# SSM preparation moved between the tiles of a feed-forward block, and a weight request moved into the down projection before it

## The chip, the cores and the metric

The kernel runs on one core of a Trainium2 chip. TensorE (PE) multiplies matrices, and its weight loads are shown apart as PEld; VectorE (DVE), ScalarE (ACT) and GpSimd (POOL) work element by element, and SyncE (SP) issues most of the DMAs. Each engine takes its own queue in order, and semaphores tie the queues together. The metric is the device time of one execution in microseconds (us); lower is better.

## What is computed

One layer of a hybrid decoder: a SwiGLU block at half weight, then a mixer in which an SSM and an attention run side by side, then a second SwiGLU block, and a last norm. 512 tokens, 1024 channels, 2816 inner channels, all float32.

```python
def swiglu(h, w_gate, w_up, w_down):
    return (jax.nn.silu(h @ w_gate) * (h @ w_up)) @ w_down

h = rms_norm(x, ffn1_norm[l])
x = x + RES_HALF * swiglu(h, ffn1_w_gate[l], ffn1_w_up[l], ffn1_w_down[l])
h = rms_norm(x, mix_norm[l])
...
x = x + y @ w_out[l]
h = rms_norm(x, ffn2_norm[l])
x = x + RES_HALF * swiglu(h, ffn2_w_gate[l], ffn2_w_up[l], ffn2_w_down[l])
```

The SSM needs matrices that depend on its parameters alone: powers of a complex decay, an input matrix, an output matrix and a matrix for short distances. The kernel works these out on the chip, beside FFN 1.

## The kernel before

**Precision.** Each float32 operand is split into a high part (`hi`, `whi`: a cast on ScalarE) and the rest (`lo`, `wlo`: a subtraction on VectorE). `mm3` (L198) makes a product of three matmuls: high by high at L200, high weight by low input at L201, low weight by high input at L202. A weight so passes a DMA to `wraw`, a cast to `whi`, a subtraction to `wlo`. `wraw`, `whi` and `wlo` have three buffers each, so a cast can start when TensorE has finished with the weight three before it.

**Groups.** Each FFN takes its 22 inner tiles in four groups, of 6, 6, 6 and 4 tiles (counted here from 1). A group first multiplies by gate and up, then `down` (L446) multiplies by the down weights in eight steps m = 0 to 7, each one 128-channel tile of `x`. `down` asks for three weights ahead; the one for step m + 3 is asked for after the matmuls of step m. After each step VectorE adds to `x` (L458), and `after(m)` runs whatever else was planned there.

**Plain tiles and pairs.** Groups 1 and 2 of FFN 1, and group 1 of FFN 2, work tile by tile, gate and up in turn: twelve tiles (0 to 11) in a group, of 24 matmuls of 512 columns each. The other groups go by `pairs` (L589): a pair is two inner tiles worked together in a fast matrix scheme of seven products in place of eight. Seven steps (n = 0 to 6), for gate and up each, of 256 columns, take combined weights and combined inputs `xq` (named b11, b21, n2, t1, t3, b22, t4 in the order of the steps). `pair_weights` (L566) loads a pair's raw weights, for gate and up one `wraw` and two `wb` each, and adds four sums `s` on GpSimd (L575). `prepare(i)` (L599) asks for these at a pair's first step, and for each step casts `whi` (L609) and subtracts `wlo` (L610). It runs two steps ahead (`AHEAD`). Before the change the first two of a group were asked for when `pairs` began, so after the whole of the down before it. FFN 1 has three pairs in group 3 and two in group 4; FFN 2 has three, three and two in its groups 2 to 4.

**Planned beside it.** `SLOTS` lists, for every place in FFN 1 where `hidden` (L401) is called, which steps of three lists are taken: `e` and `l` are the early and late steps of the SSM preparation (`prep_steps`, L704), `p` is the preparation of the pairs' inputs (`quarters`, L461). Its third line holds the twelve tiles of group 2, its fourth the first seven steps of the down behind them. VectorE's part of a slot is ordered behind the last `wlo` (`self.low`) and the last activation (`self.acted`); GpSimd's part is not. The sixteen late steps are: one that starts the tables `ec` and `es` with three squarings on VectorE; six doublings (`double`, L1039), on GpSimd, each of which needs another squaring from VectorE (all but the last); one that loads `sC`; and eight `c_powers` (L1070), by turns on GpSimd and VectorE, three operations each (`tC`, `tC`, `mC`) and a store to `kC`. In `quarters`, the two `add` steps make the sums of inputs on GpSimd (`qe`, `qd`, `q2`, `q4`), and `combos` splits them into `xu`, `xm`/`xx`, `xq`. In FFN 2 the `after` of group 1's down (L697) takes the same kind of steps, the last of them `plain("b22")` at step 5, ordered behind `self.low`.

**Order.** The program's order is a priority. A planner with a simulated timeline lays out the queue of each engine from it: what is ready on the simulated engine goes first, and among these what stands first in the program. `issue_after` forces an order on one engine. `chained` (L582) keeps the casts, and the subtractions, of the pairs in the order of the steps.

Of the kernel before, what the change touches and what calls it, by code (L numbers as in the profile page):

```python
# [20 lines left out]
KT = D // P  # L21
# [11 lines left out]
FGROUPS = {1: ((0, 6), (6, 12), (12, 18), (18, 22)), 2: ((0, 6), (6, 12), (12, 18), (18, 22))}  # L33
# [4 lines left out]
NCL = {1: 12, 2: 6}  # L38
SLOTS = ("e|e|e|e||||e"
         "|p|p|p|p|p|p|e|e|e"  # L40
         "|el|eel|eel|eel|eel|eel|eel|eep|pl|ll|epl|l"
         "|pl|pl|l|l|||")
BY_TRANSFER = 99
RELOAD = (0, 1, 0, 1, 0, 1, 0, 1)
AHEAD = 2
# [96 lines left out]
class Body:  # L142
# [250 lines left out]
    def ffn1(self):  # L393
        wgu, wd = self.d["wgu1"], self.d["wd1"]
        early, late, reload = self.prep_steps()
        prep = self.quarters(1)
        names = {"e": early, "l": late, "p": prep}
        slots = [[names[q].pop(0) for q in step] for step in SLOTS.split("|")]
        assert not early and not late and not prep

        def hidden(_=None):  # L401
            if slots:
                with ExitStack() as late:
                    for i in (self.acted, self.low):
                        if i is not None:
                            late.enter_context(self.tc.issue_after(i.ins))
                    for f in slots.pop(0):
                        f()

        hooks = {(1, 1): self.first_norm, (2, 1): self.norm_bcast}  # L410
        for f0, f1 in FGROUPS[1]:
            last = f1 == NF
            if f0 >= NCL[1]:
                acts = self.pairs(1, range((f0 - NCL[1]) // 2, (f1 - NCL[1]) // 2))
            else:
                acts, pend = [], []
                for f in range(f0, f1):
                    if f == 0:
                        pend.append(self.first_pair(1, wgu, self.xg))
                        continue  # L420
                    pair = []
                    for gu in range(2):
                        wh, wl = self.weight(wgu[f, gu].rearrange("p k m -> p (k m)"), 1024, by_transfer=f >= BY_TRANSFER)
                        ps = self.ps("gu")
                        x = self.hn if f0 else self.xg
                        for k in range(KT):
                            self.mm3(ps, wh[:, k * P:(k + 1) * P], wl[:, k * P:(k + 1) * P], x[k][0], x[k][1],
                                     k == 0, k == KT - 1)
                        pair.append(ps)
                        hooks.get((f, gu), hidden)()  # L430
                    pend.append(pair)
                    while pend and f >= max(hooks)[0]:
                        acts.append(self.activate(*pend.pop(0), normed=f0 > 0))
                if f0 == 0:
                    hidden()
            if last:
                self.prenorm(self.g_mix)
                self.reload = reload

                def hidden(m):  # L440
                    self.prenorm_tile(m)
                    if RELOAD[m]:
                        reload.pop(0)()
            self.down(wd, f0, f1, acts, hidden)

    def down(self, wd, f0, f1, acts, after):  # L446
        nf = f1 - f0
        get = lambda m: self.weight(wd[m, :, f0:f1].rearrange("p k m -> p (k m)"), nf * P)
        ws = [get(m) for m in range(3)]
        for m in range(KT):  # L450
            wh, wl = ws[m]
            ps = self.ps("dn")
            for j in range(nf):
                self.mm3(ps, wh[:, j * P:(j + 1) * P], wl[:, j * P:(j + 1) * P], acts[j][0], acts[j][1],
                         j == 0, j == nf - 1)
            if m + 3 < KT:
                ws.append(get(m + 3))
            self.added = self.nc.vector.scalar_tensor_tensor(self.x[m], ps, 0.5, self.x[m], op0=ALU.mult, op1=ALU.add)  # L458
            after(m)

# [125 lines left out]
                st.enter_context(self.tc.issue_after(self.chain[key].ins))  # L586
            self.chain[key] = f()

    def pairs(self, layer, js):  # L589
        nc = self.nc  # L590
        V, A = nc.vector, nc.scalar
        xs = ("b11", "b21", "n2", "t1", "t3", "b22", "t4")
        bank = ("a", "b", "a", "c", "a", "c", "a")
        new = (1, 1, 0, 1, 0, 0, 0)
        steps = [(j, n) for j in js for n in range(7)]
        behind = lambda: ExitStack() if (layer, j) == (2, js[-1]) else self.tc.issue_after(self.chain["V"].ins)
        ws, parts, out = {}, {}, []

        def prepare(i):  # L599
            if i >= len(steps):  # L600
                return
            j, n = steps[i]
            if n == 0:
                ws[j] = [self.pair_weights(layer, j, gu) for gu in range(2)]
            hi, lo = parts[i] = [self.wp.tile([P, 1024], F32R, name=x) for x in ("whi", "wlo")]
            for gu in range(2):
                c = slice(gu * 512, (gu + 1) * 512)
                w = ws[j][gu][n]
                self.chained("A", lambda: A.copy(hi[:, c], w))  # L609
                self.chained("V", lambda: V.tensor_tensor(lo[:, c], w, hi[:, c].bitcast(F32), op=ALU.subtract))  # L610

        for i in range(AHEAD):
            prepare(i)
        for i, (j, n) in enumerate(steps):
            prepare(i + AHEAD)
            if layer == 2 and j == (NF - NCL[2]) // 2 - 1 and n == 7 - AHEAD:
                self.tail_weights(0)
            if n == 0:
                ps = [{}, {}]
                ab = [(self.m2(name="fa"), self.m2(name="fb")) for _ in range(2)]  # L620
            hi, lo = parts.pop(i)
            for gu in range(2):
                wh, wl = (t[:, gu * 512:(gu + 1) * 512] for t in (hi, lo))
                if new[n]:
                    ps[gu][bank[n]] = self.ps("gu" + bank[n])
                o = ps[gu][bank[n]][:, 0:256]
                xh, xl = self.xq[xs[n]]
                for k in range(4):
                    self.mm3(o, wh[:, k * P:(k + 1) * P], wl[:, k * P:(k + 1) * P], xh[k], xl[k],
                             bool(new[n]) and k == 0, k == 3, skip_group_check=True)  # L630
                fa, fb = ab[gu]
                a, b, c = (ps[gu][x][:, 0:256] if x in ps[gu] else None for x in "abc")
                c11, c12, c21, c22 = fa[:, 0:256], fa[:, 256:512], fb[:, 0:256], fb[:, 256:512]
                if n == 0:
                    A.copy(c11, a)
                elif n == 1:
                    V.tensor_tensor(c11, b, c11, op=ALU.add)
                elif n == 2:
                    A.copy(c12, a)
                elif n == 3:  # L640
                    A.copy(c22, c)
                elif n == 4:
                    V.tensor_tensor(c22, a, c22, op=ALU.add)
                elif n == 5:
                    V.tensor_tensor(c12, c, c12, op=ALU.add)
                    if gu == 0:
                        A.activation(fa, fa, AF.Silu)
                    else:
                        with behind():
                            V.tensor_tensor(fa, fa, ab[0][0], op=ALU.mult)  # L650
                elif gu == 0:
                    A.activation(c21, a, AF.Silu, scale=-1.0)
                    A.activation(c22, c22, AF.Silu, scale=-1.0)
                else:
                    ga = ab[0][1]
                    with behind():
                        V.scalar_tensor_tensor(c22, c22, -1.0, ga[:, 256:512], op0=ALU.mult, op1=ALU.mult)
                        V.scalar_tensor_tensor(c21, a, -1.0, ga[:, 0:256], op0=ALU.mult, op1=ALU.mult)
            if n == 6:
                with behind():  # L660
                    out += [self.split(t) for t in ab[1]]
        return out

    def ffn2(self):
        xg, wgu, wd = self.xg, self.d["wgu2"], self.d["wd2"]
        prep, acts, pend = [], [], []
        for gi, (f0, f1) in enumerate(FGROUPS[2]):
            acts = []
            f = f0
            while f < f1:  # L670
                if f >= NCL[2]:
                    acts = self.pairs(2, range((f0 - NCL[2]) // 2, (f1 - NCL[2]) // 2))
                    break
                if f == 0:
                    pend.append(self.first_pair(2, wgu, xg))
# [23 lines left out]
                    with self.tc.issue_after(self.low.ins):  # L699
                        prep.pop(0)()  # L700

            self.down(wd, f0, f1, acts, after)

    def prep_steps(self):  # L704
        nc, cp, tp, d = self.nc, self.cp, self.tp, self.d
# [985 lines left out]
```

## Time and profile before

| what | us |
| --- | --- |
| median of three runs | 898.81 (897.58 to 899.33) |
| the profiled execution | 901.02 |
| its span, from first to last instruction | 899.1 |

| stage, from TensorE's own timeline | starts at about, us |
| --- | --- |
| FFN 1, twelve tiles of group 2 | 106 |
| down of group 2 | 180 |
| three pairs of group 3 | 215 |
| down of group 3 | 277 |
| two pairs of group 4 | 309 |
| down of group 4, then the mixer | 349 |
| FFN 2, down of group 1 | 606 |
| three pairs of group 2 | 638 |
| three pairs of group 3 | 733 |
| two pairs of group 4 | 825 |

A row of the timeline gives start, duration, engine, line, operation, output and inputs, and shapes; in brackets stands how long the engine was idle before it and who released it. SPq is SP's queue, with DMA issues. A row of the view of windows gives a stretch, its length, and the busy time of each engine with the count of its instructions; then come TensorE's granted clock (1.00 is full), the share of the DMA engines and GB/s. A row of the view of waits gives who waited for whom: total, times, longest. Durations on TensorE are modelled and overlap: a matmul of 512 columns is shown 0.39 us long, while the next one starts 0.23 us after it.

### The profile page before, as it was taken

How to read it: one execution, taken by the hardware profiler on the slowest of the kernel's cores; microseconds unless marked ns; L12 is line 12 of the kernel's file. 1: busy time of each engine (PE TensorE's matmuls, PEld its weight loads, DVE VectorE, ACT ScalarE, POOL GpSimd, SP SyncE). 2: the span in 40 equal slices, each digit the busy share in tenths (PEclk: the TensorE clock that was granted, in tenths of full speed). 3: DMA queues.
4: the chain of work that ended last, by engine and by line, in shares of the span. 5: the costliest groups of instructions: out<-in, count | busy, mean ns of one | idle time of the engine just before them, and what ended most of it. 6: DMA issues, size and time to landing. Idle time of an engine off the chain costs nothing. (4 is left out here: it accounts for less than half of the span.)

```text
span 899.1 us, 14338 instructions
## 1 busy us (share of the span) xinstructions
PE 876.8 (98%) x5400; PEld 768.8 (86%) x5400; DVE 683.8 (76%) x1253; ACT 407.8 (45%) x769; POOL 326.5 (36%) x295
## 2 busy tenths in 40 slices
PE   9999999999999999999989999999999999999996
PEld 6888887779998898888879888888899889988995
DVE  7787986597885595869887687677989569855866
ACT  7143334423553354523586443562355336533553
POOL 0133058915650450501412153182364154405402
PEclk9999999999999999999999999999999999999999
DMA  7322444455314424465201123224321442144112
GB/s 251 138 83 61 153 139 150 120 151 175 115 36 116 171 89 163 157 193 162 71 1 48 48 94 110 95 71 147 118 89 36 147 152 89 36 140 159 48 48 93
DMA packets 42116, 100.38 MB, mean 112 GB/s; under 512 B 8544, under 2 KB 10816, under 8 KB 41536
## 3 DMA queue, kind: packets, MB, share of 16 engines
q1 hardware_dynamic: 41616, 98.93, 33.5%
q8 instruction: 42, 0.69, 0.3%
q10 hardware_dynamic: 432, 0.55, 0.2%
q14 instruction: 26, 0.21, 0.1%
HBM read 91.63 MB, written 7.83 MB: 111 GB/s over the span
## 5 line engine op out<-in xcount | busy, mean ns | idle before, releaser
L163 ACT CAST whi<-wraw 128x1024 fp32r<-128x1024 f32 (+4 forms) x114 | 101.8, 899 | 194.8 <-PE dn L201 74.2
L191 DVE TENSOR_TENSOR wlo<-wraw,whi 128x1024 fp32r<-128x1024 f32 (+4 forms) x113 | 127.8, 1134 | 29.3 <-ACT whi L163 29.0
L200 PE MATMUL dn<-hi,whi 128*128 128x512 f32 (+1 forms) x336 | 127.5, 385 | 1.7 <-ACT hi L221 0.9
L201 PE MATMUL dn<-lo,whi 128*128 128x512 f32 (+1 forms) x336 | 127.8, 384 | 0.0
L202 PE MATMUL dn<-hi,wlo 128*128 128x512 f32 (+1 forms) x336 | 126.3, 384 | 1.0 <-DVE wlo L191 1.0
L575 POOL TENSOR_TENSOR s<-s,wraw 128x512 f32<-128x512 f32 x52 | 84.7, 1630 | 47.2 <-DVE x L458 24.4
L575 POOL TENSOR_TENSOR s<-wb 128x512 f32<-128x512 f32 x26 | 37.2, 1431 | 172.1 <-DMA wb<-wgs 112.6
L610 DVE TENSOR_TENSOR wlo<-s,whi 128x512 fp32r<-128x512 f32 x104 | 82.6, 839 | 12.0 <-ACT whi L609 11.7
L458 DVE SCALAR_TENSOR_TENSOR x<-dn,x 128x512 f32<-128x512 f32 x56 | 38.2, 687 | 67.4 <-PE dn L202 67.3
L609 ACT CAST whi<-s 128x512 fp32r<-128x512 f32 x104 | 59.4, 619 | 43.0 <-issue 11.9
L200 PEld LDWEIGHTS dn<-hi,whi 128*128 128x128 f32 x336 | 63.1, 188 | 14.8 <-ACT hi L221 1.3
L200 PE MATMUL gu<-hi,whi 128*128 128x512 f32 x192 | 74.1, 393 | 0.8 <-ACT hi L213 0.7
L202 PEld LDWEIGHTS dn<-hi,wlo 128*128 128x128 f32 x336 | 63.0, 188 | 13.8 <-DVE wlo L191 1.4
L201 PE MATMUL gu<-lo,whi 128*128 128x512 f32 x192 | 74.4, 390 | 0.1
L202 PE MATMUL gu<-hi,wlo 128*128 128x512 f32 x192 | 74.3, 390 | 0.0
L201 PEld LDWEIGHTS dn<-lo,whi 128*128 128x128 f32 x336 | 63.1, 188 | 12.3
L610 DVE TENSOR_TENSOR wlo<-wraw,whi 128x512 fp32r<-128x512 f32 x52 | 55.3, 1104 | 3.3 <-ACT whi L609 3.3
L287 POOL TENSOR_TENSOR sq<-sq 128x512 f32<-128x512 f32 x17 | 26.0, 1527 | 69.4 <-ACT sq L283 69.3
L200 PEld LDWEIGHTS gu<-hi,whi 128*128 128x128 f32 x192 | 36.1, 189 | 9.7 <-ACT whi L163 1.2
L609 ACT CAST whi<-wraw 128x512 fp32r<-128x512 f32 x52 | 29.2, 615 | 30.5 <-PE dn L201 30.4
L575 POOL TENSOR_TENSOR s<-wraw,wb 128x512 f32<-128x512 f32 x26 | 43.1, 1657 | 0.0
L201 PEld LDWEIGHTS gu<-lo,whi 128*128 128x128 f32 x192 | 36.1, 188 | 7.9 <-DVE lo L215 0.5
(431 smaller groups left out, 2561.8 us busy)
## 6 DMA issues: line engine op xcount, KB each, us to landing
wraw<-wd SPq DMA_DIRECT2D x48, 384.0 KB, 3.1
wraw<-wgu SPq DMA_DIRECT2D x34, 512.0 KB, 3.5
wraw<-wgs SPq DMA_DIRECT2D x26, 512.0 KB, 3.6
wb<-wgs SPq DMA_DIRECT2D x52, 256.0 KB, 5.6
wraw<-wout SPq DMA_DIRECT2D x8, 512.0 KB, 3.5
x<-xT SPq DMA_DIRECT2D x8, 256.0 KB, 4.8
kV<-mV SPq DMA_DIRECT2D x8, 256.0 KB, 2.9
kC<-mC SPq DMA_DIRECT2D x8, 256.0 KB, 4.4
```

Source lines behind the costliest of these rows:

```text
L163: return (e.copy if e is self.nc.scalar else e.tensor_copy)(out, x)
L191: self.low = self.eng("lo" + key).tensor_tensor(lo, raw, hi.bitcast(F32), op=ALU.subtract)
L200: mm(out, wh, xh, start=start, stop=False, **kw)
L201: mm(out, wh, xl, start=False, stop=False, **kw)
L202: mm(out, wl, xh, start=False, stop=stop, **kw)
L287: (eng or b.nc.gpsimd).tensor_tensor(self.acc, self.acc, sq, op=ALU.add)
L458: self.added = self.nc.vector.scalar_tensor_tensor(self.x[m], ps, 0.5, self.x[m], op0=ALU.mult, op1=ALU.add)
L575: add = lambda o, x, y: nc.gpsimd.tensor_tensor(o, x, y, op=ALU.add)
L609: self.chained("A", lambda: A.copy(hi[:, c], w))
L610: self.chained("V", lambda: V.tensor_tensor(lo[:, c], w, hi[:, c].bitcast(F32), op=ALU.subtract))
```

## The change

Two things change. First, `SLOTS`: the sixteen late steps now stand in the first eleven tiles of FFN 1's second group, two a tile in the first five, and none is left in the down behind it. The early steps and the input steps keep their places.

```diff
 SLOTS = ("e|e|e|e||||e"
          "|p|p|p|p|p|p|e|e|e"
-         "|el|eel|eel|eel|eel|eel|eel|eep|pl|ll|epl|l"
-         "|pl|pl|l|l|||")
+         "|ell|eell|eell|eell|eell|eel|eel|eepl|pl|l|epl|"
+         "|p|p|||||")
```

Second, where the next group goes by pairs, `down` now gets two calls, `then`. In steps 5 and 6, where it has no weight of its own left to ask for, it makes one of them: `prepare(0)` and `prepare(1)` of the next group. They come ahead of that step's add to `x` and of `after(m)`. `prepare` also sets `self.low` to its last subtraction.

```diff
-            self.down(wd, f0, f1, acts, hidden)
-
-    def down(self, wd, f0, f1, acts, after):
+            begun, then = self.next_pairs(1, gi)
+            self.down(wd, f0, f1, acts, hidden, then)
+
+    def next_pairs(self, layer, gi):
+        if gi + 1 == len(FGROUPS[layer]) or FGROUPS[layer][gi + 1][0] < NCL[layer]:
+            return None, None
+        js = range(*((f - NCL[layer]) // 2 for f in FGROUPS[layer][gi + 1]))
+        begun = self.pair_steps(layer, js)
+        return begun, [lambda i=i: begun[2](i) for i in range(AHEAD)]
+
+    def down(self, wd, f0, f1, acts, after, then=None):
...
             if m + 3 < KT:
                 ws.append(get(m + 3))
+            elif then and m + 1 < KT:
+                then.pop(0)()
             self.added = self.nc.vector.scalar_tensor_tensor(self.x[m], ps, 0.5, self.x[m], op0=ALU.mult, op1=ALU.add)
             after(m)
...
                 self.chained("V", lambda: V.tensor_tensor(lo[:, c], w, hi[:, c].bitcast(F32), op=ALU.subtract))
-
-        for i in range(AHEAD):
-            prepare(i)
+            self.low = self.chain["V"]
+
+        return steps, parts, prepare
+
+    def pairs(self, layer, js, begun=None):
...
+        steps, parts, prepare = begun or self.pair_steps(layer, js)
+        if not begun:
+            for i in range(AHEAD):
+                prepare(i)
         for i, (j, n) in enumerate(steps):
             prepare(i + AHEAD)
```

`ffn2` calls `next_pairs` in the same way. So five joins of a down and a group of pairs are touched, two in FFN 1 and three in FFN 2. No computation is added or left out.

More of the change, by code (lines that the diff above doesn't have):

```diff
@@ L410, in ffn1 @@
         hooks = {(1, 1): self.first_norm, (2, 1): self.norm_bcast}
-        for f0, f1 in FGROUPS[1]:
+        begun = None
+        for gi, (f0, f1) in enumerate(FGROUPS[1]):
             last = f1 == NF
             if f0 >= NCL[1]:
-                acts = self.pairs(1, range((f0 - NCL[1]) // 2, (f1 - NCL[1]) // 2))
+                acts = self.pairs(1, range((f0 - NCL[1]) // 2, (f1 - NCL[1]) // 2), begun)
             else:
@@ L587, in chained, with pair_steps @@
             self.chain[key] = f()
[L589 to L594, printed above, removed]
+    def pair_steps(self, layer, js):
+        A, V = self.nc.scalar, self.nc.vector
         steps = [(j, n) for j in js for n in range(7)]
-        behind = lambda: ExitStack() if (layer, j) == (2, js[-1]) else self.tc.issue_after(self.chain["V"].ins)
-        ws, parts, out = {}, {}, []
+        ws, parts = {}, {}
         def prepare(i):
@@ L610, in prepare @@
                 self.chained("V", lambda: V.tensor_tensor(lo[:, c], w, hi[:, c].bitcast(F32), op=ALU.subtract))
-        for i in range(AHEAD):
-            prepare(i)
+            self.low = self.chain["V"]
+        return steps, parts, prepare
+    def pairs(self, layer, js, begun=None):
+        nc = self.nc
+        V, A = nc.vector, nc.scalar
+        xs = ("b11", "b21", "n2", "t1", "t3", "b22", "t4")
+        bank = ("a", "b", "a", "c", "a", "c", "a")
+        new = (1, 1, 0, 1, 0, 0, 0)
+        out = []
+        behind = lambda: ExitStack() if (layer, j) == (2, js[-1]) else self.tc.issue_after(self.chain["V"].ins)
+        steps, parts, prepare = begun or self.pair_steps(layer, js)
+        if not begun:
+            for i in range(AHEAD):
+                prepare(i)
         for i, (j, n) in enumerate(steps):
@@ L671, in ffn2 @@
                 if f >= NCL[2]:
-                    acts = self.pairs(2, range((f0 - NCL[2]) // 2, (f1 - NCL[2]) // 2))
+                    acts = self.pairs(2, range((f0 - NCL[2]) // 2, (f1 - NCL[2]) // 2), begun)
                     break
@@ L700, in after @@
                         prep.pop(0)()
-            self.down(wd, f0, f1, acts, after)
+            begun, then = self.next_pairs(2, gi)
+            self.down(wd, f0, f1, acts, after, then)
     def prep_steps(self):
```

## The prediction, made before the changed kernel was run

> **What bounds the kernel now.** I first read the page's row of busy times: it says that TensorE is never idle for long, so only its stalls can be won.
>
> ```profile
> PE 876.8 (98%) x5400; PEld 768.8 (86%) x5400; DVE 683.8 (76%) x1253; ACT 407.8 (45%) x769; POOL 326.5 (36%) x295
> ```
>
> 899.1 - 876.8 = 22.3 us of the span are idle, and I ask which of them lie where the change works. The view of waits, cut to 179 to 280 us (FFN 1: the down of group 2, then the pairs of group 3) and to 600 to 860 us (FFN 2), names who kept TensorE waiting (total, times, longest):
>
> ```profile
> PE guc L202 <- DVE wlo L610: 1.1, 1, 1.1
> PE dn L202 <- DVE wlo L191: 1.0, 1, 1.0
> PE dn L200 <- ACT hi L221: 0.9, 1, 0.9
> PE gub L202 <- DVE wlo L610: 0.7, 2, 0.4
> ...
> PE gub L202 <- DVE wlo L610: 1.6, 2, 0.9
> PE gua L202 <- DVE wlo L610: 1.5, 1, 1.5
> ```
>
> Nearly every stall waits for VectorE's `wlo`, the low half of a weight. The timeline of TensorE shows the size of each (start, duration, in brackets the idle time):
>
> ```profile
> 183.12 0.39 PE L200 MATMUL dn<-hi,whi 128*128 128x512 f32 x1
> 183.34 0.39 PE L201 MATMUL dn<-lo,whi 128*128 128x512 f32 x1
> 184.70 0.50 PE L202 MATMUL dn<-hi,wlo 128*128 128x512 f32 x1 [0.97 <-DVE wlo L191]
> ...
> 187.95 0.50 PE L200 MATMUL dn<-hi,whi 128*128 128x512 f32 x1 [0.91 <-ACT hi L221]
> ...
> 237.91 0.39 PE L202 MATMUL gub<-xm,wlo 128*128 128x256 f32 x1 [0.32 <-DVE wlo L610]
> ...
> 242.68 0.39 PE L202 MATMUL guc<-xx,wlo 128*128 128x256 f32 x1 [1.14 <-DVE wlo L610]
> ...
> 640.20 0.38 PE L202 MATMUL gua<-xh,wlo 128*128 128x256 f32 x1 [1.51 <-DVE wlo L610]
> ```
>
> Two neighbours start 0.23 us apart (183.12, 183.34), although each is shown 0.39 long; so the bracket hides 0.16, and the first stall is 184.70 - 183.34 - 0.23 = 1.13 us. By the same rule the others cost 1.07, 0.48, 1.30 and 1.67: **5.65 us** in all. The down into the pairs of group 4, and the last two joins of FFN 2, show no stall, so an earlier request there has nothing to win.
>
> Why VectorE is late is seen in its own timeline, with GpSimd's first and last C power beside it:
>
> ```profile
> 176.34 2.70 DVE L527 TENSOR_TENSOR xu<-qd,xu 128x512 fp32r<-128x512 f32 x2
> 178.97 1.59 DVE L223 TENSOR_TENSOR lo<-a,hi 128x512 fp32r<-128x512 f32 x1
> 180.48 3.30 DVE L530 SCALAR_TENSOR_TENSOR xm<-qe,xx 128x512 fp32r<-128x512 f32 x2
> 183.70 0.95 DVE L191 TENSOR_TENSOR wlo<-wraw,whi 128x768 fp32r<-128x768 f32 x1
> ...
> 186.56 0.68 DVE L363 TENSOR_TENSOR a<-gu,s 128x512 f32<-128x512 f32 x1
> ...
> 165.63 1.11 POOL L720 TENSOR_TENSOR tC<-X,s_pwr 128x512 f32<-128x512 f32 x1
> ...
> 181.61 1.62 POOL L720 TENSOR_TENSOR mC<-tC 128x512 f32<-128x512 f32 x1
> ...
> L610 DVE TENSOR_TENSOR wlo<-s,whi x104: 673/682/1784, 215.7 to 855.1; 128x512 fp32r<-128x512 f32 x104
> ```
>
> The last row gives one operation at least, median and most: 0.68 us while GpSimd rests, 1.78 beside it. The C powers fill GpSimd until 183.2, and just then VectorE becomes free for the second down weight (183.70) and the last activation (186.56): the stalls of 1.13 and 1.07.
>
> **The change part by part.** *A. Packed steps.* Nothing is added: sixteen late steps keep their instructions, DMAs included, and move up by one to five slots. The eight C powers, every other one GpSimd's, leave tiles 9 to 11 and down steps 0 to 3 for tiles 4 to 10. Is there room? Busy time of the engines in tiles 0 to 5 and 6 to 9:
>
> ```profile
> 105.90:139.00 33.10, 33.10 (x153) 27.06 (x152) 28.86 (x98) 10.49 (x14) 14.01 (x31) 1.00 0.38 128
> 139.00:165.40 26.40, 26.40 (x175) 20.30 (x174) 12.08 (x21) 13.37 (x22) 26.07 (x28) 1.00 0.51 160
> ```
>
> The columns are PE, PEld, DVE, ACT, POOL. GpSimd has 33.1 - 14.0 = 19.1 us free in the first stretch and 0.3 in the second, and the C powers fill it up to 183.2; VectorE has 4.2 free in the first and 14.3 in the second. An order that fills 11 to 13 of the 19.1 lets GpSimd end at 170 to 172, an estimate from these rows. Then the five contended VectorE operations from 176.34 on (2.70 + 1.59 + 3.30 = 7.6 us) take 0.68 each, 4.2 us less, against the 1.13 and 1.07 that were missing: both stalls go. **A wins 2.2** (0 if GpSimd is not sooner done; below nothing in the last rival). The moved C stores stand in SP's queue ahead of weight loads; what hides them is the lead of a weight, whose price comes next.
>
> This lead is the cover of all of A:
>
> ```profile
> 112.33 1.05 ACT L163 CAST whi<-wraw 128x1024 fp32r<-128x1024 f32 x1 [5.17 <-PE gu L201]
> 123.65 1.05 ACT L163 CAST whi<-wraw 128x1024 fp32r<-128x1024 f32 x1 [2.35 <-PE gu L201]
> ...
> 113.41 1.23 DVE L191 TENSOR_TENSOR wlo<-wraw,whi 128x1024 fp32r<-128x1024 f32 x1 [1.12 <-ACT whi L163]
> ```
>
> The cast at 112.33 follows tile 0's end, when a place of the three-deep buffer comes free, so this is tile 3's weight, and its `wlo` ends at 114.64. The third cast from there, with one between, follows tile 2's end: tile 3 begins at 123.65, after 9.0 us of slack. A lag beyond that stalls TensorE one for one.
>
> [...]
>
> *B. The first pair of group 3.* GpSimd sums weights there (`s`); its first sums of pairs 0 and 1, the last of pair 1, and for comparison pair 1 of a later group; TensorE's first matmul of either group; SP's queue; VectorE:
>
> ```profile
> 207.64 1.68 POOL L575 TENSOR_TENSOR s<-wb 128x512 f32<-128x512 f32 x1 [24.41 <-DVE x L458]
> ...
> 226.21 1.30 POOL L575 TENSOR_TENSOR s<-wb 128x512 f32<-128x512 f32 x1 [5.78 <-DMA wb<-wgs]
> ...
> 237.27 1.73 POOL L575 TENSOR_TENSOR s<-s,wraw 128x512 f32<-128x512 f32 x1
> ...
> 737.99 1.29 POOL L575 TENSOR_TENSOR s<-wb 128x512 f32<-128x512 f32 x1 [8.58 <-DVE wlo L610]
> ...
> 214.84 0.28 PE L200 MATMUL gua<-xh,whi 128*128 128x256 f32 x1
> ...
> 733.08 0.28 PE L200 MATMUL gua<-xh,whi 128*128 128x256 f32 x1
> ...
> 214.00 6.78 SPq L570 DMA_DIRECT2D wraw<-wgs  x2
> 220.88 1.81 SPq L573 DMA_DIRECT2D wb<-wgs  x4
> ...
> 236.07 3.48 DVE L610 TENSOR_TENSOR wlo<-wraw,whi 128x512 fp32r<-128x512 f32 x2
> ```
>
> Pair 0's sums begin at 207.6 after 24.4 us of rest. They hold its raw weights until 220.4, so SP asks for pair 1's `wb` only from 220.9 on, and its sums run from 226.2 to 239.0, over the two `wlo` at 236.07 (1.74 each) that the stalls of 0.48 and 1.30 wait for. In the later group they start 737.99 - 733.08 = 4.9 us after its pairs begin, against 11.4 here, and that group has no stall at this boundary. With the C powers gone from GpSimd, their tiles returned and the pair asked for at down steps 5 and 6, pair 0's sums can end near 214, when the second step's `wlo` frees the raw tile anyway; pair 1's would run from about 220.5 to 233.5. **B wins 1.8** (bounds 0 and 1.8).
>
> *C. FFN 2's first join.* The queue of VectorE, and the cast whose result lay ready for `wlo`:
>
> ```profile
> 638.13 1.42 DVE L527 TENSOR_TENSOR xq<-h,xq 128x256 fp32r<-128x256 f32 x4
> 639.47 1.28 DVE L610 TENSOR_TENSOR wlo<-wraw,whi 128x512 fp32r<-128x512 f32 x2
> ...
> 630.11 1.15 ACT L609 CAST whi<-wraw 128x512 fp32r<-128x512 f32 x2 [2.79 <-PE dn L201]
> ```
>
> The four `xq` (`plain("b22")`, needed only by the pair's sixth step) stand ahead of step 0's two `wlo`. After the change the request is traced before them, and they must be issued behind its last `wlo` (`self.low`). Then `wlo` starts at 638.13 and ends at 638.81, where TensorE wants it at 640.20 - 1.67 = 638.53: about 0.35 of stall with the signal, not 1.67. What is late next is step 1's `wlo`: the same operations stand ahead of it in another order, and TensorE comes 1.3 us sooner, which costs 0.3. That wins 1.0; the boundary of the next pair, whose sums hang on step 1's raw weights and so come at the old time, can take some back, and the view of waits gave `gub`, where such boundaries stall, 1.6 us in all of FFN 2. I take **C = 0.6** (0 to 1.67).
>
> *The other joins and the added waits.* In the three other joins the request moves ahead of the adds to `x` of down steps 5 to 7; behind one waiting `wlo` stands at most one such add (0.68 us), and who waits for that is the next normalisation or the bank of `dn`, neither near. ScalarE's casts wait for TensorE's end of the down step as they did (2.79 above). Cost 0, up to one add, 0.7 us, lost.
>
> **Sum.** 2.2 + 1.8 + 0.6 = 4.6 us. The profiled execution took 901.02 us with 899.1 of span; the median of the three runs shown is 898.81. Differences carry over, as nothing outside the span changes: 899.1 - 4.6 = 894.5 of span, and **894.2 us** as the median. If every stall of A, B and C goes it is 5.65, or 893.2.
>
> **The rivals.** *1. The contention moves along.* If the 19.1 us of rest fill wholly, some 11 VectorE operations (one for each 1.75 us of GpSimd) take 1.1 longer: 12, and with one C power (2.0) 14 us. Less the 4.2 free, VectorE lags by 9.8, against 9.0 of slack: 0.8 of new stall, **895.0**. For it: the first stretch has VectorE at 28.86 of 33.1. Against: the second stretch takes up the lag.
>
> *2. The join doesn't follow.* Pair 1's `wb` stay behind a raw load in SP's queue, as at 214.00 (6.78 us for two issues), B gives nothing and C is taken back: 2.2, **896.6**.
>
> *3. The steps don't really move.*
>
> ```profile
> 139.15 0.64 POOL L720 TENSOR_TENSOR tE<-ec,q_co 128x256 f32<-128x256 f32 x1 [6.91 <-DVE q_so L720]
> ```
>
> GpSimd's longest rest in its doublings waits for VectorE's chain of squares (`q_so`), and no slot shortens this chain. GpSimd then still ends at 183, with A and B nothing: **898.2**. For it: VectorE is 87% busy there. Against: the squares of several steps can now stand in one tile.
>
> *4. Slower.* As in 3, but the order of the slots puts three C powers on GpSimd ahead of the sums for `xu` (the second `add` is in tile 8 in both). The four last from 165.63 to 183.23, 4.4 us each, so three are 13.2. The sums end where the first C power begins, 165.6, and `xu` starts at 176.34: 10.7 of cover. From there on VectorE's queue waits with `xu` at its head, with `lo`, the second down weight and the last activation behind it: 2.5 to 3.2 more on the stall of 1.13, 6.9 if the fourth is ahead too. With 0.6 from C: 898.81 + 3.2 - 0.6 = **901.4**, up to 905.1. It decides once the sums end after 176.3.
>
> **How the numbers follow.** The forecast gets 0.35, rival 1 0.15, rival 2 0.20, rival 3 0.18, rival 4 0.12. A measurement can tell about 0.2%, 1.8 us, from no change, so the bounds are 897.0 and 900.6. Faster: 0.35 + 0.15 + three quarters of rival 2 = 0.65; slower 0.12; within 0.23. The range: at the low end 893.2 less 0.7 for a boundary that eases too, 892.5; at the high end rival 3 with 1.6 for a lost add and a new small stall, 899.8. That leaves out rival 4 and some edges.
>
> **What would show it.** Right: no TensorE idle over 0.3 us in the down of group 2; GpSimd's last C power before 173; the first sum of pair 0 before 203 and of pair 1 before 222; the four `xq` behind `wlo` at the first join of FFN 2. Rival 1: idle brackets in tiles 3 to 6 with `wlo L191`. Rivals 3 and 4: C powers past 180, in 4 with `xu` waiting for `qd`. The prediction is wrong if TensorE's order itself changes, or if the stalls go and the span does not shrink by them.

## The result, and the profile after

The changed kernel takes **903.07 us** (median of 6 runs, 901.73 to 905.05) against 898.46 (897.15 to 899.81) for the kernel before on the same chip: a ratio of **1.0051**, 95% interval 1.0036 to 1.0067. The prediction was 894.2. The change is slower by 4.6 us, where 4.6 had been forecast as a gain.

The profiled execution of the changed kernel took 902.21 us with a span of 900.3. That of before, at 901.02, lay 2.6 us above the median of these runs, and this one lies 0.9 below its own, so the two spans differ by 1.2 us only. I therefore compare stages, each from TensorE's first `dn` or `gua` matmul in it to the first one of the next stage. Beside them stands the kernel request_only from below, whose `SLOTS` are those of before and whose profile is near its median:

| stage, us | before | request_only | after |
| --- | --- | --- | --- |
| down of group 1 and the twelve tiles of group 2 | 106.23 | 106.23 | 114.29 |
| down of group 2 | 35.13 | 35.11 | 32.64 |
| pairs of group 3 | 61.75 | 61.25 | 59.98 |
| pairs of FFN 2's group 2 | 62.13 | 62.29 | 61.28 |

So 8.06 us are lost in one stage, and 5.1 won in the next ones. The page's row of busy times answers to the one shown of before:

```profile
PE 874.9 (97%) x5400; PEld 769.4 (85%) x5400; DVE 694.8 (77%) x1253; ACT 407.6 (45%) x769; POOL 330.5 (37%) x295
```

The instruction counts are the same, but VectorE is busy for 11.0 us more (694.8 - 683.8). The view of waits, for tiles 0 to 11, then for the down of group 2 with group 3, then for FFN 2:

```profile
PE tV L962 <- DVE aB L740: 7.0, 1, 7.0
...
PE gub L202 <- DVE wlo L616: 0.5, 1, 0.5
...
PE gub L202 <- DVE wlo L616: 1.2, 2, 0.7
PE guc L202 <- DVE wlo L616: 0.5, 1, 0.5
PE gua L202 <- DVE wlo L616: 0.2, 1, 0.2
```

The two stalls of the down are gone, those of the first pair of group 3 too, and FFN 2's first join has 0.2 left of 1.5. In their place stands one wait of 7.0 us that the prediction does not mention. TensorE's timeline and its granted clock there:

```profile
154.22 1.09 PE L962 MATMUL tV<-cst,aB 128*128 128x128 f32 x4 [7.01 <-DVE aB L740]
154.96 0.78 PE L200 MATMUL gu<-xh,whi 128*128 128x512 f32 x1
...
157.62 0.39 PE L200 MATMUL gu<-xh,whi 128*128 128x512 f32 x1
```
```profile
156.00:157.00 1.00, 1.00 (x4) 0.81 (x3) 1.00 (x2) 0.00 (x0) 1.00 (x2) 0.50 0.30 49
157.00:158.00 1.00, 1.00 (x5) 0.81 (x4) 1.00 (x2) 0.00 (x0) 1.00 (x2) 0.72 0.63 233
```

`tV` are transposes of the SSM's input matrix (`matv`). They are small, but they stand in TensorE's one queue between two tiles, and whatever they wait for holds all matmuls behind them, here for 7.0 us. After the wait the granted clock (third from the right) is 0.50, up to about 157.6; the six matmuls from 154.96 to 157.62 take 2.66 us, where the same six take some 1.5 at full clock (0.32 for the first behind transposes, 0.23 for each other). That is 1.2 us more, which with the 7.0 makes up the loss of 8.06 to 0.2.

What made `aB` late is read from the queues of VectorE, ScalarE and SyncE. Before the change, VectorE:

```profile
131.74 0.69 DVE L363 TENSOR_TENSOR a<-gu,s 128x512 f32<-128x512 f32 x1 [0.23 <-ACT s L361]
...
136.23 0.68 DVE L720 TENSOR_TENSOR aB<-tB 128x512 f32<-128x512 f32 x1
```

`aB` ended at 136.91, and TensorE came to its `tV` at about 147.4: a lead of 10.5 us. After the change, VectorE, then ScalarE, then SyncE's queue:

```profile
135.24 3.21 DVE L191 TENSOR_TENSOR wlo<-wraw,whi 128x1024 fp32r<-128x1024 f32 x2
143.47 0.69 DVE L363 TENSOR_TENSOR a<-gu,s 128x512 f32<-128x512 f32 x1 [5.02 <-ACT s L361]
146.50 1.76 DVE L740 TENSOR_TENSOR tB<-bbar,p_pwr 128x512 f32<-128x512 f32 x1
...
152.87 1.21 DVE L740 TENSOR_TENSOR aB<-tB 128x512 f32<-128x512 f32 x1
```
```profile
141.04 0.73 ACT L1086 ACTIVATE X<-sC,cst 128x512 f32<-128x512 f32 x1 [4.89 <-DMA sC<-sC]
...
142.86 0.58 ACT L361 ACTIVATE s<-gu 128x512 f32<-128x512 f32 x1
```
```profile
136.48 0.33 SPq L185 DMA_DIRECT2D wraw<-wgu  x1
136.86 1.18 SPq L1084 DMA_DIRECT2D sC<-sC  x2
```

`aB` ends at 154.08, 17.2 us later than before, against a lead of 10.5. One sees a chain through four in-order queues: the `sC` loads stand behind a weight load; ScalarE stands 4.9 us at `X`, which wants `sC`; the Silu (`s`) stands behind `X`, VectorE's `a` waits for the Silu, and the step's VectorE work (`tB`, `aB`), forced behind `a` by `issue_after`, then runs at 1.2 to 1.8 us an operation beside GpSimd.

### The profile page after: what moved, and what is told of

Read it like the earlier page. It is cut to its first block, busy times and chain, and to the rows that moved or that the text cites. A ratio compares the mean times of both kernels' runs of the same rounds, so it can differ in the third digit from the quotient of the medians.

```text
span 900.3 us, 14349 instructions
## 1 busy us (share of the span) xinstructions
PE 874.9 (97%) x5400; PEld 769.4 (85%) x5400; DVE 694.8 (77%) x1253; ACT 407.6 (45%) x769; POOL 330.5 (37%) x295
## 5 line engine op out<-in xcount | busy, mean ns | idle before, releaser
L191 DVE TENSOR_TENSOR wlo<-wraw,whi 128x1024 fp32r<-128x1024 f32 (+4 forms) x113 | 131.8, 1170 | 14.9 <-ACT whi L163 14.5
L616 DVE TENSOR_TENSOR wlo<-s,whi 128x512 fp32r<-128x512 f32 x104 | 85.1, 864 | 9.6 <-ACT whi L615 9.4
L616 DVE TENSOR_TENSOR wlo<-wraw,whi 128x512 fp32r<-128x512 f32 x52 | 52.2, 1044 | 3.3 <-ACT whi L615 3.3
```

Of the source, the lines that this page charges most:

```text
L191: self.low = self.eng("lo" + key).tensor_tensor(lo, raw, hi.bitcast(F32), op=ALU.subtract)
```

## The experiments

Ratios are against the kernel before on the same chip, with 95% intervals.

**1 and 2. Each half of the change alone.** slots_only is the kernel before with the new `SLOTS`; request_only is the changed kernel with the old ones:

```diff
-         "|ell|eell|eell|eell|eell|eel|eel|eepl|pl|l|epl|"
-         "|p|p|||||")
+         "|el|eel|eel|eel|eel|eel|eel|eep|pl|ll|epl|l"
+         "|pl|pl|l|l|||")
```

> The kernel before with the changed kernel's SLOTS alone; the weights are asked for as before. In the changed kernel's trace TensorE stands 7.0 us at tile 7 of FFN 1's second group (tV waits for VectorE's aB), the down of group 2 begins some 8 us later than before and then takes 2.5 us less. Theory S (the packed steps make the loss, all of it in that stall): the stall of about 7 us is here too, the down of group 2 has none over 0.3 us, and the time is 898.5 + 8 - 2.5 = 904.0, less 0 to 1.8 if pair 1 of group 3 has its sums sooner without the earlier request: 902.2 to 904.0. Rival R (the earlier request, by another order that the planner then finds for VectorE and ScalarE, makes the loss): no stall over 1 us at tile 7, and 896.3 (2.2 us from the two stalls of the down).

> The changed kernel with the SLOTS of before; only the first two weights of a group of pairs are asked for inside the down. Theory S: nothing is lost; FFN 2's first join wins the 0.85 us that the changed kernel's trace shows there, the stalls of 1.13 and 1.07 us in the down of group 2 stay, pair 1 of group 3 wins 0 to 1.8: 895.9 to 897.7. Rival R: the time is that of the changed kernel, 902 to 904, with a stall of several us near tile 7 of group 2 or in a join.

slots_only: 904.07, 1.0055 (1.0042 to 1.0068), with the same stall of 7.0 us and 8.5 us lost in that stage. request_only: 899.12, 0.9997 (0.9989 to 1.0006), no stall there. So Theory S holds: the packing makes the whole loss. The request alone can't be told from no change; its time lies above the 895.9 to 897.7 that were expected of it. The pairs of group 3 take 59.48 us in slots_only, without the request, and 61.25 in request_only, so what looks like B's gain came with the packing.

The order of the queues says why. In the traces of before and of request_only TensorE, ScalarE, GpSimd and SyncE take the same operations in the same order, by their names and shapes, through the whole program. VectorE does too, but for one place: at FFN 2's first join two `wlo` now stand ahead of the four `xq`. The same place is all that tells the changed kernel's queues from those of slots_only. So of the five joins that the request was to touch, one was changed, and in FFN 1 it moved nothing.

**3 and 4. The wait at the head of ScalarE's queue.** load_early moves the two `sC` loads to the first late step; xy_gpsimd takes `X` and `Y` off ScalarE:

```diff
             S.rho, S.ec, S.es = (cp.tile([P, NP, NCH], F32, name=n, tag="rce", bufs=3) for n in ("rho", "ec", "es"))
+            st["pq"] = pq = [S.m2(name="sC") for _ in range(2)]
+            for i in range(2):
+                nc.sync.dma_start(pq[i], d["sC"][:, i])
```
```diff
-            nc.scalar.activation(x0, pq[0], AF.Copy, scale=S.sgn)
-            nc.scalar.mul(y0, pq[1], -1.0)
+            G.tensor_scalar(x0, pq[0], S.sgn, None, op0=ALU.mult)
+            G.tensor_scalar(y0, pq[1], -1.0, None, op0=ALU.mult)
```

> The changed kernel, with the two sC loads moved from the step that makes X and Y to the first late step. In the changed kernel ScalarE's X stands 4.9 us at the head of ScalarE's queue for the sC load, with the Silu of tile 7 behind it, VectorE's a behind that, and aB and TensorE's tV behind a. Theory H (the wait at the head of ScalarE's queue makes the stall): X starts about 4.9 us sooner, the stall goes from 7.0 to about 2, and the time from 903.1 to about 898. Rival B (VectorE is behind by then, by the packed squares beside GpSimd's work, and X only waits in its shadow; or tV waits for another step's tile): the stall stays at 5 to 7 us and the time at 902 to 904.

> The changed kernel, with X and Y made by GpSimd in place of ScalarE, so that no wait for the sC load stands in ScalarE's queue; GpSimd gets two operations of about 1 us more, behind the doublings. Theory H: the Silu of tile 7 follows the cast of about 134.9 at once, 5 to 6 us sooner than in the changed kernel; the stall goes from 7.0 to 1 to 2 us and the time to 897 to 898.5. Rival B (the Silu waits for a cast that is itself late, and VectorE is behind): the stall stays over 3 us and the time over 900.

load_early: 899.48, 1.0000 (0.9987 to 1.0014); the wait at `tV` fell from 7.0 to 0.7 us. xy_gpsimd: 901.98, 1.0030 (1.0017 to 1.0043); the Silu of that tile started at 136.37 and not at 142.86, and no wait over 0.6 us was left at that `tV`. So the head of ScalarE's queue did make that stall, as Theory H says. The times followed in part: load_early wins back most of the loss (1.0051 to 1.0000), xy_gpsimd less (1.0030), and neither reaches the 897 to 898.5 of Theory H, as another stall came. TensorE, ScalarE and SyncE of load_early:

```profile
148.74 0.63 PE L962 MATMUL tV<-cst,aB 128*128 128x128 f32 x4 [0.65 <-DVE aB L740]
...
158.49 0.43 PE L993 MATMUL qp<-aB,cbr 128*32 128x128 f32 x8 [2.43 <-ACT s L361]
```
```profile
156.38 0.63 ACT L974 ACTIVATE ncbi<-cbi 128x512 f32<-128x512 f32 x1 [13.34 <-DMA cbi<-sCbd]
...
157.85 0.59 ACT L361 ACTIVATE s<-gu 128x512 f32<-128x512 f32 x1
```
```profile
151.27 0.33 SPq L1103 DMA_DIRECT2D kC<-mC  x1
...
152.13 0.45 SPq L973 DMA_DIRECT2D cbi<-sCbd  x1
```

The pattern is the same one queue further: SyncE stands at the store of the first C power until GpSimd has made it, the `cbi` load stands behind the store (152.13; before the change 138.98), ScalarE stands 13.3 us at `ncbi`, and the next Silu behind it lets TensorE wait 2.4 us at `qp`, the next small matmuls. xy_gpsimd waits 3.2 us there and 3.8 at the last `tV`.

**5 and 6. The store out of SyncE's queue.** kc_gpsimd is load_early with GpSimd's own stores issued by GpSimd:

```diff
-                nc.sync.dma_start(keep[1][:, g8 * 512:(g8 + 1) * 512], o)
+                (nc.gpsimd if e is G else nc.sync).dma_start(keep[1][:, g8 * 512:(g8 + 1) * 512], o)
```

> The kernel load_early, with the kC stores of GpSimd's four C powers issued by GpSimd, behind its own mC, and not by SyncE. In load_early SyncE's queue stands at the first kC store until 151.27, when GpSimd's first mC is done; the cbr and cbi loads stand behind it (151.7, 152.1; before the change 138.5, 139.0), ScalarE stands 13.3 us at ncbi for cbi, and the next weight's cast and the Silu behind ncbi hold TensorE for 2.8 us. Theory Q (in-order queues hand the late mC on): the loads of cbr and cbi go before 146, the stall of 2.8 us goes, and the time falls by 2 to 3 us from load_early's 899.5 to about 897. Rival P (the loads wait for a free scratch tile, not for the store ahead of them): the loads still go after 149, the stall stays and the time is 899 to 900.

> The kernel kc_gpsimd once more, for a trace at full clock. By Theory Q the loads of cbr and cbi go before 146 and TensorE does not wait at qp; by Rival P they go after 149. Its time was 901.0, not the 897 of Theory Q, so a wait over 1 us is expected at a later point of tiles 8 to 11.

kc_gpsimd: 900.96, 1.0012 (1.0004 to 1.0021). Its queues are read from a second run of the same kernel, kc_gpsimd_2 (901.34):

```profile
139.66 0.37 SPq L973 DMA_DIRECT2D cbr<-sCbd  x1
140.13 0.37 SPq L973 DMA_DIRECT2D cbi<-sCbd  x1
```
```profile
PE gu L202 <- DVE wlo L191: 1.5, 1, 1.5
PE dn L202 <- DVE wlo L191: 1.3, 1, 1.3
```

Theory Q is right about the loads (139.7, not after 149) and about `qp`, which no longer waits. It is wrong about the time. The late VectorE now shows itself at the next weight (1.5 us), and 1.3 us of stall are back in the down. Removing one wait after another uncovers the next consumer of the same lateness.

**7 and 8. C powers on VectorE.** In load_early and in request_only:

```diff
-            late.append(c_powers(g8, (G, V)[g8 % 2]))
+            late.append(c_powers(g8, V))
```

> The kernel load_early with all eight C powers on VectorE, none on GpSimd. Theory V (VectorE loses as much to GpSimd's work beside it as it would take to do that work itself): twelve operations of 0.69 us, 8.3 us, are added to VectorE, and twelve on GpSimd of 1.6 to 2.1 us, some 20 us, go, beside which VectorE's operations take 1.5 to 1.8 and not 0.69 us: VectorE is not later, sums for xu are done some 10 us sooner, no stall over 1 us is left at tiles 7 to 11 and the time is 896 to 898. Rival W (the work itself is what makes VectorE late): stalls of 2 us and more at tiles 8 to 11 or in the down of group 2, and 900 to 904.

> The kernel request_only (SLOTS of before, earlier request of the weights) with all eight C powers on VectorE. Theory V: from 165 us on GpSimd has only sums left, xu, lo and the second down weight take 0.68 us an operation, the two stalls of 1.13 and 1.07 us in the down of group 2 go and so do the two of the first pair of group 3: 899.1 - 2.2 - 1.8 = 895.1. Rival W: VectorE's 8.3 us more push xu, lo and the last activation back, the stalls stay or grow, and the time is 899 to 902.

load_cpow_v: 901.80, 1.0026 (1.0015 to 1.0036), with waits of 0.9, 1.1 and 3.0 us at `tV`, `qp` and `tV`. req_cpow_v: 902.37, 1.0036 (1.0023 to 1.0049). Both times lie in Rival W's range, but only load_cpow_v speaks against Theory V. In req_cpow_v the two stalls of the down are gone, as Theory V has it, and the time is lost behind the down. SyncE, GpSimd and TensorE there:

```profile
207.83 0.94 SPq L584 DMA_DIRECT2D wb<-wgs  x2
...
213.96 1.29 POOL L586 TENSOR_TENSOR s<-wb 128x512 f32<-128x512 f32 x1 [47.28 <-DMA wb<-wgs]
...
223.08 0.58 PE L200 MATMUL gua<-xq,whi 128*128 128x256 f32 x1 [3.71 <-ACT fa L654]
```

GpSimd has nothing to do for 47 us, and pair 0's sums still begin 6.3 us later than before the change: the `wb` loads stand in SyncE's queue behind a raw load (206.25) and a C store (207.45). The casts of the sums come late, ScalarE's `fa` stands behind them, and TensorE waits 3.7 us for it.

**9 and 10. The two halves of the packing.** pack_dbl packs only the doublings; mild packs only `sC` and the C powers, by one to three slots:

```diff
-         "|ell|eell|eell|eell|eell|eel|eel|eepl|pl|l|epl|"
-         "|p|p|||||")
+         "|ell|eell|eell|eel|ee|ee|ee|eep|pl|ll|epl|l"
+         "|pl|pl|l|l|||")
```
```diff
+         "|el|eel|eel|eel|eel|eel|eell|eepl|pll|ll|epl|l"
+         "|pl|p|||||")
```

> The changed kernel, of whose packing only the doublings stay: they stand two a tile in tiles 0 to 2 and one in tile 3, while the sC load, X, Y and the C powers are back in their old places. The queues of TensorE and of SyncE are those of request_only. Theory L (the loss comes from sC, X, Y and the C powers, which now stand in the queues of SyncE, ScalarE and VectorE ahead of what tiles 6 to 9 need): no stall over 1 us in tiles 0 to 11, and since GpSimd is done with its doublings some 8 us sooner, the stalls of 1.13 and 1.07 us in the down go as in the changed kernel: 899.1 - 2.2 - 0 to 1.8 = 895 to 897. Rival D (the packed squares beside GpSimd's doublings make VectorE late, and this alone holds tV): a stall of 3 us and more at tiles 5 to 8 and 900 to 903.

> The changed kernel with the other half of the packing: the doublings stand one a tile as before, and sC and the C powers one to three slots sooner than before the change (sC in tile 6, the C powers from tile 7 on, one of them left in the down). Theory L: the C powers now stand ahead of the sums for xu on GpSimd, which has no free time before, and sC, X, Y ahead of the Silu and the cast: a stall of 2 us or more in tiles 8 to 11 or in the down of group 2, 900 to 903. Rival D: without packed squares nothing is late in tiles 5 to 8, and with the C powers out of the down the time is 896 to 898.

pack_dbl: 900.67, 1.0016 (1.0004 to 1.0028). mild: **896.69, 0.9970** (0.9959 to 0.9980), faster than both kernels. Theory L falls: the C powers, which it took for harmful, win 0.3% when they move a little, and the doublings, with the queues of TensorE and SyncE as in request_only, lose. Rival D holds in part: pack_dbl's time is the forecast one, but its stall at `tV` is 1.0 us and not over 3. The 7.0 us are seen only where the doublings are packed and `X` stands in ScalarE's queue for its load. mild moves the C powers by three slots at most, the changed kernel by five, so mild doesn't show what their full move costs alone. Busy times from 106 to 184 us (columns: length, then PE, PEld, DVE, ACT, POOL, clock, DMA) of before, after, pack_dbl and mild, in this order:

```profile
106.00:184.00 78.00, 77.73 (x407) 61.91 (x405) 56.39 (x130) 29.38 (x44) 57.59 (x71) 1.00 0.42 132
```
```profile
106.00:184.00 78.00, 70.99 (x374) 57.36 (x373) 66.78 (x131) 27.61 (x42) 62.98 (x71) 0.96 0.44 141
```
```profile
106.00:184.00 78.00, 76.99 (x404) 61.48 (x403) 63.15 (x128) 28.75 (x44) 60.99 (x71) 1.00 0.43 132
```
```profile
106.00:184.00 78.00, 78.00 (x409) 62.50 (x408) 57.48 (x131) 29.73 (x44) 58.42 (x71) 1.00 0.48 145
```

VectorE has the same work in all four (128 to 131 instructions), but is busy for 56.4 us before, 66.8 after, 63.2 in pack_dbl and 57.5 in mild; GpSimd, with 71 each, for 57.6, 63.0, 61.0 and 58.4. With the doublings packed, VectorE's squares and weights and GpSimd's doublings run side by side and both take longer. pack_dbl has the waits that this alone makes:

```profile
PE dn L202 <- DVE wlo L191: 1.2, 1, 1.2
...
PE tV L962 <- DVE aB L740: 1.0, 1, 1.0
PE dn L200 <- ACT hi L221: 0.9, 1, 0.9
```

mild has no wait over 0.5 us from tile 0 to the end of group 3, its `aB` is as early as before, and the down takes 33.72 us, the pairs of group 3 60.48. But its win is not the one that term A worked out. VectorE, GpSimd and TensorE of mild:

```profile
176.63 1.86 DVE L191 TENSOR_TENSOR wlo<-wraw,whi 128x768 fp32r<-128x768 f32 x1
...
180.72 2.51 DVE L538 TENSOR_TENSOR xu<-qd,xu 128x512 fp32r<-128x512 f32 x2
...
182.76 1.62 POOL L740 TENSOR_TENSOR mC<-tC 128x512 f32<-128x512 f32 x1
...
190.23 0.98 PE L200 MATMUL dn<-hi,whi 128*128 128x512 f32 x3
```

GpSimd's last C power ends at 184.4, later than before (183.2), and the last activation comes at 188.84, not at 186.56. What differs is the order. The `wlo` of the second down weight now stands ahead of `xu` on VectorE (176.63; before 183.70, behind it), and the planner lets TensorE take other matmuls of the down first and those that want the last activation later (three `hi` matmuls in a row at 190.23). Which of the two wins more, no run separates.

**11 to 13. GpSimd's end.** These ask whether GpSimd's end sets the stalls of the down. req_dbl_v is request_only, mild_dbl_v is mild, with the last doubling on VectorE; pack_dbl_load is pack_dbl with load_early's edit:

```diff
                 cb, sb = bc(c, n), bc(s, n)
+                E = V if 2 * n == NCH else G
...
-                tt(v[0], e, cb, ALU.mult, G)
+                tt(v[0], e, cb, ALU.mult, E)
```

> The kernel request_only (SLOTS of before) with the last doubling, six operations of 512 columns, on VectorE and not on GpSimd. In the trace of before VectorE is busy for 9.2 of the 24 us from 142 to 166, where GpSimd has no rest; these six take GpSimd 1.5 to 2.0 us each and would take VectorE 0.69. If what holds the down of group 2 is GpSimd's end at 183 alone, GpSimd ends some 9 us sooner, at 174, the stalls of 1.13 and 1.07 us go and pair 1's sums come sooner: 895 to 897. Rival: the four us more on VectorE delay wlo or aB at tiles 6 to 8 and the stall only moves: 899 to 901.

> The kernel mild with the last doubling on VectorE. GpSimd's doublings end at 143 and not at 152, so its last C power should end near 175 and not at 184, xu and the last activation come sooner, and the small waits that mild's down of group 2 still has (33.7 us against 32.64 without any) go: 895 to 896. If the four us more on VectorE at 142 to 150 make it late there, a stall at tiles 7 to 9 eats this: 897 to 898.

> The kernel pack_dbl with the two sC loads moved to the first late step. In pack_dbl GpSimd rests 5 us before its first C power, until ScalarE's X at 165.6, and ends at 184. With X sooner it should start at 161.7 and end at 179. If GpSimd's end decides the stalls in the down, they fall from 1.4 and 1.07 us to under 0.5 together and the time from 900.7 to 898.5 or less. If they hang on something else (the order in which VectorE takes xu and lo), they stay and the time is 900 to 901.

req_dbl_v: 898.07, 0.9984 (0.9976 to 0.9993): a gain, but a small one: of the stalls of 1.13 and 1.07 us in the down, 0.55 and 1.07 stay. GpSimd, which has its doublings done 9 us sooner, still waits for `X` at 164.3 and ends at 182.2. mild_dbl_v: 896.18, 0.9976 (0.9967 to 0.9986), not to be told from mild; GpSimd ends at 179.0 and the down takes 33.34 us. pack_dbl_load: 898.82, 1.0002 (0.9993 to 1.0010); GpSimd ends at 181.6 instead of 184.3, and the down falls from 35.41 to 33.60 us: the larger stall goes, 0.8 us of the other stays.

**14. mild without the request.**

> The kernel before with the SLOTS of mild alone; the weights are asked for as before. If the earlier request is worth nothing, as with the SLOTS of before (ratio 0.9997), the time is mild's, 896 to 897, with a stall at FFN 2's first join of 1.6 us that comes back as smaller ones in mild. If B's and C's gains need the request, pair 1 of group 3 has its stalls of 0.5 and 1.3 us back and the time is 898 to 899.

897.57, 0.9985 (0.9976 to 0.9994). The pairs of group 3 take 60.55 us against 60.48 with the request, so what is won there needs no request. The stall of FFN 2's first join is back (1.67 us), and FFN 2's first pairs take 61.87 against 61.30. The request, which again moves only those two `wlo`, seems to be worth something in mild (0.9970 against 0.9985), but the intervals touch.

## Why the prediction was wrong, step by step

**The reading of before was right.** The five stalls are there, each goes or shrinks under some edit, and mild wins some 2.5 us, most of it in the down of group 2 and in group 3 (94.20 us together against 96.36 in request_only).

**Term A failed, at the step "This lead is the cover of all of A".** I asked what a late VectorE would hold up, found a weight with 9.0 us of slack, and set a lag of 9.8 us at most against it. The lead was not the error, as `tV` had even more, 10.5. The lag was: 17.2 us, not 9.8. load_early, which has no stand for `sC`, splits it in three:

```profile
137.22 0.68 DVE L363 TENSOR_TENSOR a<-gu,s 128x512 f32<-128x512 f32 x1
...
147.00 3.10 DVE L740 TENSOR_TENSOR aB<-tB 128x512 f32<-128x512 f32 x2
```

Its first `aB` ends at about 148.6, 11.7 us later than before. `a` is 5.5 us later, because `X` and `Y` stand ahead of the Silu and the squares of the packed doublings ahead of `a`; `tB` and `aB` behind it take 6.2 us more, at 1.5 to 1.8 us each beside GpSimd; the 5.5 us that the changed kernel is later still go with ScalarE's stand at `X`. The second, and a part of the first, are rival 1, the contention that moves along, which came, at a higher price than its 0.8 us. The third I had not seen at all: I had weighed the moved DMAs as something that makes weights late in SyncE's queue, and not as something that another engine waits for at the head of its queue.

**A's premise failed too.** GpSimd's last C power was to end at 170 to 172 us. After the change:

```profile
105.90:139.00 33.10, 33.10 (x153) 27.05 (x152) 29.70 (x100) 9.04 (x12) 21.38 (x39) 1.00 0.39 123
```
```profile
178.76 2.00 POOL L740 TENSOR_TENSOR mC<-tC 128x512 f32<-128x512 f32 x1
```

Of the 19.1 us of rest 7.4 were filled (21.38 - 14.01), not 11 to 13, and the end came at 180.8, only 2.5 sooner.

**And yet both stalls went, for the wrong reason.** TensorE arrives later, and the down shows no stall once it does:

| kernel | down of group 2 begins | GpSimd's last C power ends | down takes, us |
| --- | --- | --- | --- |
| before | 179.7 | 183.2 | 35.13 |
| pack_dbl | 180.5 | 184.3 | 35.41 |
| kc_gpsimd_2 | 183.2 | 184.7 | 34.25 |
| load_early | 184.9 | 183.6 | 32.64 |
| after | 187.3 | 180.8 | 32.64 |
| mild | 179.8 | 184.4 | 33.72 |

load_early ends GpSimd's powers no sooner than before and has no stall in the down either. The 2.5 us "won" are the shadow of the 7 us lost: the stall moved forward and was paid at a higher price. My sign for A, no idle over 0.3 us in this down, was met and proved nothing; the one on GpSimd's end (before 173) was the honest one, and failed. mild, in the last row, shows that GpSimd's end isn't the only lever either: TensorE comes as early as before, GpSimd ends later, and the down is 1.4 us shorter, by the other order of `wlo` and `xu` and of TensorE's matmuls.

**Term B failed at the step that the earlier request lets the sums run sooner.** In FFN 1 the request moved no operation. What moved the first sum is the packing: it starts at 196.43 in slots_only and at 207.82 in request_only. GpSimd's sums and SyncE's queue after the change:

```profile
195.01 1.29 POOL L586 TENSOR_TENSOR s<-wb 128x512 f32<-128x512 f32 x1 [14.25 <-DMA wb<-wgs]
207.44 1.29 POOL L586 TENSOR_TENSOR s<-s,wraw 128x512 f32<-128x512 f32 x1 [11.14 <-issue]
...
225.88 1.29 POOL L586 TENSOR_TENSOR s<-wb 128x512 f32<-128x512 f32 x1 [7.43 <-DMA wb<-wgs]
...
203.90 2.29 SPq L581 DMA_DIRECT2D wraw<-wgs  x2
...
210.82 8.57 SPq L581 DMA_DIRECT2D wraw<-wgs  x3
219.44 1.85 SPq L584 DMA_DIRECT2D wb<-wgs  x4
```

The first sum is 12.6 us sooner than before, but the second comes at 207.44, and pair 1's begin at 225.88 against 226.21. They are hardly sooner; TensorE, 5.1 us later at the pairs, finds them ready. That is rival 2, the join that doesn't follow. The second sum is the first one that needs the raw weight: its load goes at 203.90, behind the last two down weights in SyncE's queue (199.16), and lands 3.4 us later, just ahead of the sum. Pair 1's `wb` stand behind raw loads until 219.44. In mild pair 1's sums begin at 222.3, and its stalls of 0.48 and 1.30 us are down to 0.3 and 0.5, with no late TensorE.

**Term C was right as a mechanism.** VectorE and TensorE of the changed kernel at FFN 2's first join:

```profile
639.73 1.28 DVE L616 TENSOR_TENSOR wlo<-wraw,whi 128x512 fp32r<-128x512 f32 x2
640.93 1.42 DVE L538 TENSOR_TENSOR xq<-h,xq 128x256 fp32r<-128x256 f32 x4
```
```profile
640.46 0.39 PE L202 MATMUL gua<-xh,wlo 128*128 128x256 f32 x1 [0.17 <-DVE wlo L616]
```

The four `xq` stand behind `wlo` now, and 0.33 us of stall are left where 0.35 had been worked out. Later boundaries take back a part, as I had said: the pairs of FFN 2's group 2 take 61.87 to 62.13 us in the three kernels without the request, and 61.25 to 62.48, with 61.66 in the middle, in the twelve with it. The 0.6 that I took is anything from 0.2 (the middle) to 0.6 (mild) and 0.9 (the changed kernel) in these, and nothing in request_only (62.29).

**Sum.** In place of -2.2 - 1.8 - 0.6 stands, in the profiles: +8.06 in tiles 0 to 11, -2.49 and -1.77 in the two stages in its shadow, -0.85 in FFN 2, in all +2.95. Code that the change doesn't touch, from the down of group 4 to FFN 2's first down, took 256.97 us in the profile of before and 255.53 after, which hides 1.44 of it in the spans. In that of before the granted clock is 0.91 in the stretches from 440 to 460 and from 480 to 500 us; after, it is 1.00 in both. The stages place 2.95 us of the 4.6 by which the medians differ, a little less than the 3.2 at the lower end of the interval; where the rest lies, no stage shows. Rivals 3 and 4 did not come: the doublings moved (they end 8 us sooner), and `xu` is 6.6 us later (182.92) but ahead of a TensorE that is later still. That the time falls into rival 4's 901.4 to 905.1 is luck: VectorE never stands at `xu`. One sign of being wrong that the prediction names did come: the packing changed TensorE's order. Before, the small matmuls `qp` stand in four lots of sixteen, from 154.79 on; after, 48 of them come in a row from 164.63 on. What this costs, no run separates.

## What to carry to other kernels

Before moving work forward, list every queue in which it stands with a wait (a DMA's consumer on another engine, a small matmul between large ones), and add up the lags along that chain. An engine's idle time was not free room here, as another engine slowed down beside it: with the steps packed 71 GpSimd instructions went from 57.6 to 63.0 us and some 130 of VectorE from 56.4 to 66.8. A stall that vanishes behind a new stall is not won; test each gain with TensorE on time. And compare the order of the queues before and after: here half of the change altered one place in the whole program.

## What the runs showed of the hardware beyond this

**Two paces of the same matmul.** In the pairs, matmuls of 256 columns start either about 118 or about 113 ns apart, with the clock granted in full. In FFN 2 they stay at one pace for tens of microseconds; in the profile of before one turn stands at a short wait for a weight (663 us), others, at about 750 and 858 us, at none. In the profile of before, from 743 and from 763 us on, TensorE is busy throughout:

```profile
743.00:753.00 10.00, 10.00 (x87) 9.91 (x86) 9.33 (x10) 3.59 (x9) 7.78 (x5) 1.00 0.01 2
...
763.00:773.00 10.00, 10.00 (x90) 10.00 (x89) 8.87 (x10) 5.70 (x13) 9.84 (x7) 1.00 0.01 2
```

The same ten microseconds hold 87 matmuls or 90. Over a pair, 168 matmuls, this is some 0.8 us, more than the 0.6 that C was to win; why the pace changes stays open.

**The clock after a stall.** The wait of 7.0 us was followed by a granted clock of 0.50 up to about 157.6, which cost another 1.2 us. In load_early a wait of 2.4 us was followed by a clock of 0.92 and 0.74 in two stretches of 5 us, from 155 and from 160 (together 0.34 of 5 us, or 1.7 us of full clock), while one of 3.2 in xy_gpsimd and one of 1.5 in kc_gpsimd_2 left it at 1.00. The later wait of 3.8 in xy_gpsimd was followed by 0.97 and 0.69, again 1.7 us of full clock. So the length of the wait alone didn't decide: 2.4 us were enough in one place and 3.2 were not in another. What did, no run shows.

**Small operations beside GpSimd.** VectorE's squares are 128x16: in the changed kernel a `q_b` takes 0.18 us at 130.37 and 0.56 us at 132.70, beside GpSimd's operations of 256 columns. That is some 0.4 us more on a very short operation; one of 128x512, `tB`, goes from 0.69 before (133.73) to 1.76 here (146.50), and to 1.79 in load_early (145.29).
